# Prefix log-sum-exp over time: tiles of three time steps per partition instead of two, Exp written over its input, all tiles as one stream of chunks, and a last store in parts

## The chip, the cores and the metric

The kernel runs on one core of one Trainium2 chip. The metric is the device time of one execution in microseconds, as the median of several runs. The profile is one profiled execution on the same core.

## The reference

The input x has the shape (4, 4096, 4128) in float32: 4 batches, 4096 time steps, 4128 columns. For each batch and column the output is the running log-sum-exp over time:

```python
out[:, 0, :] = x[:, 0, :]
for t in range(1, S):
    mx = np.maximum(out[:, t - 1, :], x[:, t, :])
    out[:, t, :] = mx + np.log(np.exp(out[:, t - 1, :] - mx) + np.exp(x[:, t, :] - mx))
```

That is the logarithm of a running sum of exp(x). Input and output are 270.5 MB each, and both cross between HBM and the on-chip memory SBUF once.

## The kernel before

A tile is 256 consecutive time steps of one batch with all 4128 columns. It lies in SBUF as 128 partitions, each of which holds R = 2 consecutive time steps of 4128 columns, 33,024 bytes in one run. There are 16 tiles for each batch, 64 in all, and they are worked in order. A tile is loaded by one DMA (line 102) and stored by one DMA (line 153), both issued by SP, the sync engine. Five buffers `xt` hold tiles.

The columns of a tile are cut into four chunks of 1024; the last chunk also carries the 32 columns that are left over, called the tail. A chunk c goes through these steps in class `Step`:

- `exp(c)` (line 111): ScalarE (ACT) takes Exp of both time steps of the chunk and writes fp16 into a buffer `et`.
- `head(c)`: TensorE (PE) sums over the partitions with matmuls by constant 128x128 matrices. `incl` (a triangle with its diagonal) takes the first time step of every partition, `excl` (a triangle without it) the second, and `pick` adds the running sum that the tile before left in `carry[c]`. The result in `pt` (PSUM, the memory that PE writes) is the running sum at the first time step of each partition. Each chunk takes two matmuls of 512 columns for each matrix, line 86.
- `ln(0, c)` (line 126): ACT takes Ln of `pt` and writes it over `xt`, where the first time step was.
- `second(c)`: PE adds the second time step to `pt` by the unit matrix `ident`.
- `close(c)`: ACT takes Ln for the second time step, and then `keep` (lines 90 and 91) on VectorE (DVE) stores the last 32 partitions of `pt` as an fp16 value and an fp16 remainder in `carry[c]`. Two DVE instructions.

The tail has its own small matmuls (`tail_mm`), Ln (line 149) and carry.

The order is written out by hand in `run` and in the loop at the end. Within a tile, a chunk's Exp and head come one chunk ahead of the Ln of the chunk before. Between tiles nothing overlaps in this order: a tile's first Exp follows the last Ln of the tile before. On SP, three loads come first. For each tile i, the load of tile i + 3 is then issued ahead of the store of tile i. With five buffers that load waits until the store of tile i - 2 has ended.

Every matmul is issued with its own weight load (PEld in the profile).

Of the kernel before, what the change touches and what calls it, by code (L numbers as in the profile page):

```python
# [7 lines left out]
FP32 = mybir.dt.float32  # L8
FP16 = mybir.dt.float16
ACT = mybir.ActivationFunctionType  # L10
P = 128
R = 2
CH = 1024
MM = 512
HI, LO = 96, 32


def _constants(nc, pool):


    def tri(base, name):
        t = pool.tile([P, P], FP16, name=name)
        nc.gpsimd.memset(t, 1.0)

        nc.gpsimd.affine_select(  # L25
            out=t, in_=t, pattern=[[1, P]], compare_op=mybir.AluOpType.is_ge,
            fill=0.0, base=base, channel_multiplier=-1,
        )
        return t

    def ones_where_zero(bases, step, name):
        t = pool.tile([P, P], FP16, name=name)
        nc.gpsimd.memset(t, 0.0)
        for base in bases:
            nc.gpsimd.affine_select(  # L35
                out=t, in_=t, pattern=[[step, P]], compare_op=mybir.AluOpType.not_equal,
                fill=1.0, base=base, channel_multiplier=1,
            )
        return t

    return (
        tri(0, "incl"),
        tri(-1, "excl"),
        ones_where_zero([0], -1, "ident"),
        ones_where_zero([-(HI + 31), -(LO + 31)], 0, "pick"),
    )


@with_exitstack
def kernel(  # L50
    ctx: ExitStack,
    tc: tile.TileContext,
    x: bass.AP,
    out: bass.AP,
):

    nc = tc.nc
    B, S, D = x.shape  # L60
    rows = P * R
    n_t = S // rows
    assert S % rows == 0
    n_main = D // CH
    tail = D - n_main * CH
    t0 = n_main * CH

    nc.scalar.preload_act_table_set("natural_log_exp_and_others")  # L68
    consts = ctx.enter_context(tc.tile_pool(name="consts", bufs=1))
    incl, excl, ident, pick = _constants(nc, consts)  # L70

    xpool = ctx.enter_context(tc.tile_pool(name="xpool", bufs=5))
    epool = ctx.enter_context(tc.tile_pool(name="epool", bufs=4))
    cpool = ctx.enter_context(tc.tile_pool(name="cpool", bufs=1))
    pmain = ctx.enter_context(tc.tile_pool(name="pmain", bufs=3, space=bass.MemoryType.PSUM))
    ptail = ctx.enter_context(tc.tile_pool(name="ptail", bufs=2, space=bass.MemoryType.PSUM))

    carry = [cpool.tile([P, CH], FP16, name=f"carry{c}") for c in range(n_main)]
    carry_t = cpool.tile([P, tail], FP16, name="carry_t")
    for t in (*carry, carry_t):  # L80
        nc.vector.memset(t, 0.0)  # L81

    ctx.enter_context(tc.manual_schedule())

    def mm(pt, w, rhs, start, stop):
        nc.tensor.matmul(pt, lhsT=w, rhs=rhs, start=start, stop=stop, skip_group_check=True)  # L86

    def keep(cr, pt):

        nc.vector.tensor_copy(cr[HI:HI + 32, :], pt[HI:HI + 32])  # L90
        nc.vector.tensor_tensor(  # L91
            out=cr[LO:LO + 32, :], in0=pt[HI:HI + 32], in1=cr[HI:HI + 32, :],
            op=mybir.AluOpType.subtract,
        )

    class Step:
        def __init__(self, b, k):
            self.first = k == 0
            self.xt = xpool.tile([P, R, D], FP32, name="xt")
            self.et, self.pt = {}, {}  # L100
            self.dram = lambda t: t[b, k * rows:(k + 1) * rows, :].rearrange("(p j) d -> p j d", j=R)
            nc.sync.dma_start(out=self.xt, in_=self.dram(x))  # L102

        def cols(self, c):
            return slice(c * CH, (c + 1) * CH if c + 1 < n_main else D)

        def exp(self, c):
            s = self.cols(c)
            w = s.stop - s.start
            et = epool.tile([P, R, CH + tail], FP16, name="et")  # L110
            nc.scalar.activation(et[:, :, :w], self.xt[:, :, s], ACT.Exp)  # L111
            self.et[c] = et

        def head(self, c):
            et = self.et[c]
            pt = self.pt[c] = pmain.tile([P, CH], FP32, name="pt")
            for s in range(0, CH, MM):
                mm(pt[:, s:s + MM], incl, et[:, 0, s:s + MM], True, False)
            for s in range(0, CH, MM):
                mm(pt[:, s:s + MM], excl, et[:, 1, s:s + MM], False, self.first)  # L120
            if not self.first:
                for s in range(0, CH, MM):
                    mm(pt[:, s:s + MM], pick, carry[c][:, s:s + MM], False, True)

        def ln(self, j, c):
            nc.scalar.activation(self.xt[:, j, c * CH:(c + 1) * CH], self.pt[c], ACT.Ln)  # L126

        def second(self, c):
            pt = self.pt[c]
            for s in range(0, CH, MM):  # L130
                mm(pt[:, s:s + MM], ident, self.et[c][:, 1, s:s + MM], False, True)

        def close(self, c):

            self.ln(1, c)
            keep(carry[c], self.pt[c])

        def tail_mm(self):
            et = self.et[n_main - 1]
            qt = self.qt = ptail.tile([P, R, tail], FP32, name="qt")  # L140
            e0, e1 = et[:, 0, CH:], et[:, 1, CH:]
            for j in range(R):
                mm(qt[:, j, :], incl, e0, j == 0, False)
                mm(qt[:, j, :], incl if j else excl, e1, False, self.first)
                if not self.first:
                    mm(qt[:, j, :], pick, carry_t, False, True)

        def ln_tail(self):
            nc.scalar.activation(self.xt[:, :, t0:D], self.qt, ACT.Ln)  # L149
            keep(carry_t, self.qt[:, 1, :])  # L150

        def store(self):
            nc.sync.dma_start(out=self.dram(out), in_=self.xt)  # L153

        def run(self):
            last = n_main - 1
            self.exp(0)
            self.head(0)
            for c in range(1, n_main):
                self.exp(c)  # L160
                self.head(c)
                if c == last:
                    self.tail_mm()
                self.ln(0, c - 1)
                self.second(c - 1)
                if c >= 2:
                    self.close(c - 2)
            self.ln(0, last)
            self.second(last)
            self.close(last - 1)  # L170
            self.ln_tail()
            self.close(last)
            self.store()

    work = [(b, k) for b in range(B) for k in range(n_t)]
    ahead = 3
    steps = []
    for i, (b, k) in enumerate(work):
        if i == 0:
            steps += [Step(*work[n]) for n in range(ahead)]  # L180
        if i + ahead < len(work):
            n = i + ahead
            steps.append(Step(*work[n]))
        steps[i].run()


# [28 lines left out]
```

The softmax here doesn't subtract the row's maximum and nothing guards it: scores larger than these inputs give would overflow.

## Time and profile before

| what | value |
|---|---|
| median of 9 runs | 1265.41 us (1264.98 to 1266.11) |
| the profiled execution's own time | 1265.23 us |
| its span in the trace | 1263.4 us |
| bytes read and written | 270.53 MB each, 428 GB/s over the span |
| ACT busy | 962.4 us (76%), 833 instructions |
| PE busy | 660.6 us (52%), 2392 matmuls, and 2392 weight loads |
| DVE busy | 655.7 us (52%), 645 instructions |
| Exp of a chunk (128x2048) | 1904 ns each, 192 of them |
| Ln of a chunk's time step (128x1024) | 1028 ns each, 512 of them |
| `keep`, two instructions (32x1024) | 1230 and 1226 ns |
| a load | 4128 KB, 29.4 us from issue to landing |
| a store | 4128 KB, 38.9 us from issue to landing |

The span runs from the first to the last event of the trace; the execution's own time has a little more around it. A busy share says how much of the span an engine worked, and not whether it was waited for. A load's or a store's time from issue to landing holds its wait in the queue: 16 DMA engines share each transfer, and transfers issued earlier come first.

### The profile page before, as it was taken

How to read it: one execution, taken by the hardware profiler on the slowest of the kernel's cores; microseconds unless marked ns; L12 is line 12 of the kernel's file. 1: busy time of each engine (PE TensorE's matmuls, PEld its weight loads, DVE VectorE, ACT ScalarE, POOL GpSimd, SP SyncE). 2: the span in 40 equal slices, each digit the busy share in tenths (PEclk: the TensorE clock that was granted, in tenths of full speed). 3: DMA queues.
4: the chain of work that ended last, by engine and by line, in shares of the span. 5: the costliest groups of instructions: out<-in, count | busy, mean ns of one | idle time of the engine just before them, and what ended most of it. 6: DMA issues, size and time to landing. Idle time of an engine off the chain costs nothing.

```text
span 1263.4 us, 7025 instructions
## 1 busy us (share of the span) xinstructions
PE 660.6 (52%) x2392; PEld 242.4 (19%) x2392; DVE 655.7 (52%) x645; ACT 962.4 (76%) x833; POOL 2.2 (0%) x13
## 2 busy tenths in 40 slices
PE   2565655545545465464454655546445464554641
PEld 1222221211112121121121211112112121121210
DVE  3565565464454554545546455454564544545443
ACT  6889887778778787786877877778778787787872
POOL 0000000000000000000000000000000000000000
PEclk9878778777687776877767777777777787777776
DMA  9999999999999999999999999999999999999997
GB/s 401 417 433 433 429 432 434 429 431 430 433 434 433 433 432 433 429 433 431 434 434 433 435 428 432 431 435 430 434 435 434 433 433 431 429 433 431 434 434 328
DMA packets 18466, 541.51 MB, mean 429 GB/s; under 512 B 2048, under 2 KB 2048, under 8 KB 2048
## 3 DMA queue, kind: packets, MB, share of 16 engines
q1 hardware_dynamic: 18432, 541.07, 99.5%
q8 instruction: 19, 0.31, 0.1%
q14 instruction: 15, 0.12, 0.0%
HBM read 270.53 MB, written 270.53 MB: 428 GB/s over the span
## 4 chain that ended last, share of the span: by engine, by line
DMA 82%; ACT 1%; SPq 1%; DVE 1%; issue 1%; PE 0%; ACTq 0%
DMA out_dram<-xt 80%; DMA xt<-in_x_dram 2%; SPq L102 1%; ACT xt L126 1%; ACT et L111 1%; DVE carry L90 0%; DVE carry L91 0%; PE pt L86 0%; SPq L153 0%; DVE carry_t L90 0%; DVE carry_t L91 0%; ACTq L126 0%
## 5 line engine op out<-in xcount | busy, mean ns | idle before, releaser
L90 DVE CAST carry<-pt 32x1024 f16<-32x1024 f32 x256 | 314.8, 1230 | 574.7 <-ACT xt L126 571.4
L111 ACT ACTIVATE et<-xt 128x2048 f16<-128x2048 f32 (+1 forms) x256 | 485.5, 1921 | 152.4 <-DMA xt<-in_x_dram 152.4
L126 ACT ACTIVATE xt<-pt 128x1024 f32<-128x1024 f32 x512 | 504.4, 1028 | 124.5 <-PE pt L86 63.7
L86 PE MATMUL pt<-et,incl 128*128 128x512 f16 x512 | 210.9, 504 | 550.0 <-ACT et L111 375.2
L91 DVE TENSOR_TENSOR carry<-pt,carry 32x1024 f16<-32x1024 f32 x256 | 314.0, 1226 | 8.9
L86 PE MATMUL pt<-et,excl 128*128 128x512 f16 x512 | 210.9, 504 | 0.0
L86 PEld LDWEIGHTS <-incl 128*128 128x128 f16 x704 | 69.1, 111 | 684.0 <-issue 632.6
L86 PE MATMUL pt<-carry,pick 128*128 128x512 f16 x480 | 194.9, 498 | 0.0
L86 PE MATMUL pt<-et,ident 128*128 128x512 f16 x512 | 172.6, 422 | 28.3 <-ACT xt L126 28.3
L86 PEld LDWEIGHTS <-excl 128*128 128x128 f16 x576 | 71.0, 123 | 115.6 <-issue 82.9
L86 PEld LDWEIGHTS <-pick 128*128 128x128 f16 x600 | 69.7, 118 | 94.5 <-issue 66.0
L86 PEld LDWEIGHTS <-ident 128*128 128x128 f16 x512 | 49.5, 106 | 102.0 <-issue 75.5
L86 PE MATMUL qt<-et,incl 128*128 128x32 f16 x192 | 19.6, 189 | 0.0
L86 PE MATMUL qt<-carry_t,pick 128*128 128x32 f16 x120 | 15.6, 182 | 0.0
L149 ACT ACTIVATE xt<-qt 128x64 f32<-128x64 f32 x64 | 14.6, 227 | 0.0
L90 DVE CAST carry_t<-qt 32x32 f16<-32x32 f32 x64 | 12.6, 196 | 2.0
L91 DVE TENSOR_TENSOR carry_t<-qt,carry_t 32x32 f16<-32x32 f32 x64 | 12.4, 193 | 2.2
L86 PE MATMUL qt<-et,excl 128*128 128x32 f16 x64 | 11.6, 182 | 0.0
L81 DVE MEMSET carry<- 128x512 uint32 x4 | 1.9, 485 | 1.1 <-PEq L199 1.0
L68 ACT ACT_TABLE_LOAD x1 | 1.3, 1283 | 0.8 <-PEq L199 0.8
L35 POOL TENSOR_SCALAR_AFFINE_SELECT pick<-pick 128x128 f16<-128x128 f16 x2 | 0.6, 292 | 0.1
L25 POOL TENSOR_SCALAR_AFFINE_SELECT incl<-incl 128x128 f16<-128x128 f16 x1 | 0.3, 292 | 0.0
(11 smaller groups left out, 1.9 us busy)
## 6 DMA issues: line engine op xcount, KB each, us to landing
xt<-in_x_dram SPq DMA_DIRECT2D x64, 4128.0 KB, 29.4
out_dram<-xt SPq DMA_DIRECT2D x64, 4128.0 KB, 38.9
```

Of the source, the lines that this page charges most:

```text
L25: nc.gpsimd.affine_select(out=t, in_=t, pattern=[[1, P]], compare_op=mybir.AluOpType.is_ge, fill=0.0, base=base, channel_multiplier=-1,)
L35: nc.gpsimd.affine_select(out=t, in_=t, pattern=[[step, P]], compare_op=mybir.AluOpType.not_equal, fill=1.0, base=base, channel_multiplier=1,)
L68: nc.scalar.preload_act_table_set("natural_log_exp_and_others")
L81: nc.vector.memset(t, 0.0)
L86: nc.tensor.matmul(pt, lhsT=w, rhs=rhs, start=start, stop=stop, skip_group_check=True)
L90: nc.vector.tensor_copy(cr[HI:HI + 32, :], pt[HI:HI + 32])
L91: nc.vector.tensor_tensor(out=cr[LO:LO + 32, :], in0=pt[HI:HI + 32], in1=cr[HI:HI + 32, :], op=mybir.AluOpType.subtract,)
L102: nc.sync.dma_start(out=self.xt, in_=self.dram(x))
L111: nc.scalar.activation(et[:, :, :w], self.xt[:, :, s], ACT.Exp)
L126: nc.scalar.activation(self.xt[:, j, c * CH:(c + 1) * CH], self.pt[c], ACT.Ln)
L149: nc.scalar.activation(self.xt[:, :, t0:D], self.qt, ACT.Ln)
```

## The change

- A partition of a tile holds R = 3 consecutive time steps, a run of 49,536 bytes. A batch's 32 rows of 128 are ten tiles of three and one of two. In the first batch the tile of two comes first, in the others last. There are 44 tiles: 40 of three and 4 of two.
- Exp is written as fp16 over the first half of the chunk's own place in `xt`. The pool of `et` buffers is gone, and `xt` has four buffers of three rows.
- The chunks of all tiles are one list, 176 chunks. In turn g of one loop come: for chunk g - 2 the third Ln with `keep`, for chunk g - 1 the second Ln and the next `ident` matmuls, for chunk g the first Ln and its `ident` matmuls, then the Exp of chunk g + 2 and the head of chunk g + 1. This holds across the border of two tiles. A tile of two rows has two Ln, and `keep` follows the second.
- `head` takes the first row by `incl` and the other two by `excl`.
- `mm` gives `ldweights=False` where the matrix is the one of the matmul before.
- SP issues four loads first. Later a load follows a store: after the store of tile i comes the load of tile i + 3, into the buffer whose store was that of tile i - 1.
- The last store goes out as three DMAs, of partitions 0 to 4, 5 to 79 and 80 to 127.

```diff
-R = 2
+R = 3
+UNEVEN = ((0, 5), (5, 80), (80, P))
...
-    xpool = ctx.enter_context(tc.tile_pool(name="xpool", bufs=5))
-    epool = ctx.enter_context(tc.tile_pool(name="epool", bufs=4))
+    bufs = 4
+    xpool = ctx.enter_context(tc.tile_pool(name="xpool", bufs=bufs))
...
+    held = [None]
+
+    def mm(pt, w, rhs, start=False, stop=False):
+
+        if held[0] is not w:
+            nc.tensor.matmul(pt, lhsT=w, rhs=rhs, start=start, stop=stop, skip_group_check=True)
+            held[0] = w
+            return
+        pe = nc.tensor
+        pe.add_instruction(mybir.InstMatmult(
...
+            start_tensor_calc=start, stop_tensor_calc=stop, ldweights=False,
...
+        def store(self, parts=((0, P),)):
+            for a, b in parts:
+                nc.sync.dma_start(out=self.dram(out)[a:b], in_=self.xt[a:b])
...
+        def exp(self):
+            c0, w = self.c * CH, self.w
+            nc.scalar.activation(
+                self.t.half[:, :, 2 * c0:2 * c0 + w], self.t.xt[:, :, c0:c0 + w], ACT.Exp,
+            )
...
+        def stage(self, j):
+
+            t, c, pt = self.t, self.c, self.pt
+            nc.scalar.activation(t.xt[:, j, c * CH:(c + 1) * CH], pt, ACT.Ln)
+            if j + 1 < t.r:
+                for s in range(0, CH, MM):
+                    mm(pt[:, s:s + MM], ident, self.e(j + 1, s, s + MM), stop=j + 2 == t.r)
+                if c == last and j == 0:
+                    nc.scalar.activation(t.xt[:, :, t0:D], self.qt, ACT.Ln)
+                    keep(carry_t, self.qt[:, t.r - 1, :])
+            else:
+                keep(carry[c], pt)
...
+    ahead = bufs - 1
+    for s in steps[:bufs]:
+        s.load()
+    stored = 0
+    chunks[0].exp()
+    chunks[1].exp()
+    chunks[0].head()
+    for g in range(len(chunks) + R - 1):
+        for d in range(R - 1, -1, -1):
+            if 0 <= g - d < len(chunks) and d < chunks[g - d].t.r:
+                k = chunks[g - d]
+                k.stage(d)
+                if k.c == last and d + 1 == k.t.r:
+                    k.t.store(UNEVEN if k.t is steps[-1] else ((0, P),))
+                    if bufs <= stored + ahead < len(steps):
+                        steps[stored + ahead].load()
+                    stored += 1
+        if g + 2 < len(chunks):
+            chunks[g + 2].exp()
+        if g + 1 < len(chunks):
+            chunks[g + 1].head()
```

## The prediction

> **What bounds the kernel now.** I read the page's slices and queues first, then the chain that ended last, then the last 70 us in order of time, then short stretches of the end.
>
> ```profile
> DMA  9999999999999999999999999999999999999997
> GB/s 401 417 433 433 429 432 434 429 431 430 433 434 433 433 432 433 429 433 431 434 434 433 435 428 432 431 435 430 434 435 434 433 433 431 429 433 431 434 434 328
> ...
> q1 hardware_dynamic: 18432, 541.07, 99.5%
> ...
> DMA out_dram<-xt 80%; DMA xt<-in_x_dram 2%; SPq L102 1%; ACT xt L126 1%; ACT et L111 1%; DVE carry L90 0%; DVE carry L91 0%; PE pt L86 0%; SPq L153 0%; DVE carry_t L90 0%; DVE carry_t L91 0%; ACTq L126 0%
> ```
>
> All 16 DMA engines are full except in the first and last slice, and the chain is one store after another. ACT at 76% of the span, PE and DVE at 52% lie under it. The bytes do not change, so only three things can move the time: how fast a full DMA engine moves its bytes, a gap in the queue, and the end. The chain in order of time shows the end:
>
> ```profile
> 1193.82 29.40 DMA xt<-in_x_dram
> 1223.24 1.92 ACT et L111
> ```
>
> The last load lands at 1223.2 (call it T). SP's timeline then has the last store issued at 1240.15 (T + 16.9), while three older stores keep the queues full. Short stretches after that (columns: stretch, length, busy us of PE, PEld, DVE, ACT, POOL, clock, DMA share, GB/s):
>
> ```profile
> 1242.00:1252.00 10.00, 0.00 (x0) 0.00 (x0) 2.53 (x3) 0.00 (x0) 0.00 (x0) 0.50 1.03 446
> 1252.00:1254.00 2.00, 0.00 (x0) 0.00 (x0) 0.00 (x0) 0.00 (x0) 0.00 (x0) 0.50 0.69 297
> 1254.00:1256.00 2.00, 0.00 (x0) 0.00 (x0) 0.00 (x0) 0.00 (x0) 0.00 (x0) 0.50 0.69 297
> 1256.00:1258.00 2.00, 0.00 (x0) 0.00 (x0) 0.00 (x0) 0.00 (x0) 0.00 (x0) 0.50 0.31 132
> 1258.00:1260.00 2.00, 0.00 (x0) 0.00 (x0) 0.00 (x0) 0.00 (x0) 0.00 (x0) 0.50 0.12 50
> 1260.00:1262.00 2.00, 0.00 (x0) 0.00 (x0) 0.00 (x0) 0.00 (x0) 0.00 (x0) 0.50 0.04 17
> ```
>
> The engines do not stop together. In the trace's packet records, the last store's 16 completion packets fall so: five within 0.2 us, ten 2.4 to 6.5 us later, one 9.05 us after the first. This slow engine lost its 9 us over the whole run, some 0.14 us with each store. It never idles, and it ends at T + 39.3 (four times 9.76 us, the spacing of its DMAs), 0.9 us before the span's end.
>
> **What the Trainium skill says.** "DMA: Bandwidth & Descriptors", section Latency and other measured facts, calls engines 7 and 15 usually slower than the rest; here one engine of the 16 is. Its section on why a DMA increments its semaphore by 16 says that a transfer uses the largest k up to 16 that divides the partitions, on the lowest-numbered engines. The trace of before has 16 completion packets for each of its 128-partition DMAs, and no other k. The sections Where 436 GB/s comes from and How a descriptor splits into AXI transactions give prices below. "TensorE: Matmul & The Clock Gate" says that weight loads may run ahead of matmuls; here they do (PEld overlaps PE), so they are no wall time.
>
> **Part 1: runs of 49.5 KB.** DMAs fall from 128 to 88 full ones and three parts of one. Each engine still does 8 packets for each DMA. A full engine of before spends 9.757 us for 8 x 33,024 B; at the page's 27.2 GB/s an engine (435/16) the bytes alone are 9.713, so 0.044 us per DMA is overhead, and 40 fewer DMAs give -1.7 us. Against it: a row is 16,512 B, so two rows are 129 x 256 B, but three are 193.5 x 256 B, and every odd partition's run starts off a 256 B boundary. By the page this costs 4 beats of 32 B, 4.7 ns; four odd packets in each of 80 three-row DMAs make +1.5 us. The trace of before has only aligned runs. Bounds: 0 (the write side sets the pace) to +3.0 (both sides pay). I take +1.0. Sum: -0.7.
>
> **Part 2: one stream of chunks.** Three-row tiles need per chunk an Exp of 128x3072, by 1.5 x 1904 ns (the 128x2048 row) 2.86 us, and three Ln at 0.97 (pairs in the timeline take 1.93). Four chunks and the tail's Ln make 23.4 us of ACT per tile, and a load and a store take 2 x 14.6 = 29.2: hidden, with 6 us over. DVE's `keep` pairs fall from 256 to 176, 80 x 2.46 = 197 us less, all off the path. fp16 over x drops the et pool; loads now also wait for PE, whose reads end before the store that they wait for anyway. Cost 0.
>
> What the stream does add: ACT runs Exp two chunks ahead, so Exp of the next tile's first chunk stands before the last six Ln of this tile, and waits for the next load. A store now waits for the landing of the next tile. Worked along ACT's order: three Exp, seven Ln and the tail's Ln, 8.6 + 6.8 + 0.2 = 15.6 us after that landing. The slow engine then still has a store and a load before it, 29.2 us: no gap. The fast ones, 9 us ahead, need it 20.2 us after the landing less 1.3 us for a DMA to start (first issue 0.80, first packet 2.1): still in time. SP issues a load behind a store now; queued behind its wait is only the next store, which is not ready.
>
> **Part 3: held operands.** In the program as built, PE has 2,268 matmuls and still 2,268 weight loads, one for each; `ldweights=False` leaves none out. The 124 pairs fewer come from the three-row tiling. Cost 0, and were they gone, it would be 0 too: PE waits for ACT (375 us of its idle time before the incl matmuls).
>
> **Part 4: four loads up front.** Four loads are 23.2 MB, 54 us of queue. The first store waits for Exp of tile 1 and is ready near 37 us (landing 28.0, two Exp, four Ln), the second near 58: no gap, 0.
>
> **Part 5: the end.** Last come load 43 (two rows), stores 41, 42 (three rows) and 43 (two rows): 8 rows after the landing T, as before. But store 42 now waits for T: three Exp of 1.90, seven Ln and the tail's Ln, 5.7 + 6.8 + 0.2 = 12.7 us, and 1.3 to start. The fast engines are through store 41 at T - 9.05 + 14.6 = T + 5.6 (some 1.5 later if it too comes late to them, as the short load 43 before it makes it) and idle until T + 14.0; all but the slow one then start together and end store 42 at T + 28.6. Store 43 is issued near T + 24: in time by 3 us. Its parts of 5, 75 and 48 partitions use k = 5, 15 and 16 engines: engines 0 to 4 get 9 rows of 1.22 us, 5 to 14 get 8, engine 15 gets 3. If 15 is the slow one it ends at T + 29.2 + 3.7 = T + 32.9; the first five end last, at T + 28.6 + 11.0 = **T + 39.6**, against T + 39.3. So +0.3: what the split takes from the slow engine has been lost by the others' wait for store 42. T itself moves with part 1 and with the slow engine.
>
> Slow engine's own loss: 9 us before; bounds -3 (its delay is per packet, and packets fall by a third) to +1. I take 0.
>
> **Sum.** -1.7 + 1.0 + 0.3 = -0.4 us on the profiled execution's 1265.23 (span 1263.4 and 1.8 around it). The median of the runs shown is 1265.41, 0.2 above it. So **1264.9 us**.
>
> **Rivals.**
> - A, the slow engine loses per packet: -2.8 (9 us x 40/128), T comes earlier by it: 1262.1. For it: the delay sits in short extra times of single packets, all on stores. Against: such extra times may follow the work beside them, which lasts as long. Chance 0.13.
> - B, the split works as it is meant to: store 42 is issued early enough, nobody idles, and the last is the latest of the middle ten, T - 9.05 + 6.5 + 39.0 = T + 36.4, 2.9 before T + 39.3; with -0.7 of part 1, 1261.8. It needs store 42 some 8 us sooner than ACT's order gives. Chance 0.12.
> - C, slower: the odd partitions' runs. Each engine moves 320 of them. To be slower by 2.5 us they must eat 2.5 + 1.7 - 0.3 = 3.9 us, 12 ns each; from there it decides. At 16 ns (14 beats) it is 1265.4 - 1.7 + 5.1 + 0.3 = 1269.1. For it: stores of 128 B leftovers at both ends are not in the trace. Against: 14 beats is over three times the page's price. Chance 0.18.
> - D, compute too slow for the end: between the last two landings ACT has 14.6 + 9.8 = 24.4 us for 23.4 of work. An Exp over its own input of 3.5 us would take 26.0 and miss by 1.6; in store 42's chain its three two-row Exp are 2.33 instead of 1.90, 1.3 more: 1267.8. For it: no row shows Exp writing over its input. Against: 3.5 is 22% over the row. Chance 0.15; half of it is inside 0.2%.
> - Else my own case, 0.42, from 1262.5 to 1267.5.
>
> **How the numbers follow.** A measurement of this kernel tells a difference over about 0.2% (2.5 us) from none. Faster: A, B and a little of mine, 0.27. Slower: C, half of D and a little of mine, 0.31. Same: 0.42. The range reaches from 1260.0 (A and B partly together) to 1269.5 (C): cases of both signs; mine alone is 1262.5 to 1267.5.
>
> **What would show it.** DMA packets 8 per engine and DMA of 1.83 us each; 2,268 weight loads; a wait of the last full store for ACT after the last landing, with DMA's share falling 20 to 30 us before the end instead of only in the last 10; store 42 issued 12 to 13 us after that landing. A DMA spacing on a full engine over 14.65 us speaks for C, a slow engine that is under 7 us late for A, a last store that starts with the queues still full for B. The forecast is wrong if the time leaves 1260 to 1269.5, or if a gap opens in the middle of the run.

## The result, and the profile after

The changed kernel takes **1271.61 us** (median of 9 runs, 1271.39 to 1272.07) against 1265.39 us before (29 runs): a ratio of 1.0050, 95% interval 1.0042 to 1.0058. It is 6.2 us slower. The forecast was 1264.9 us, with a range from 1260.0 to 1269.5.

The page of the kernel after, with the lines that answer to those of before (engines' busy time, DMA share and rate by slice, the data queue, the chain by line):

```profile
PE 691.1 (54%) x2268; PEld 237.5 (19%) x2268; DVE 451.5 (36%) x445; ACT 947.3 (75%) x733; POOL 2.2 (0%) x13
...
DMA  9999999999999999999999999999999999999987
GB/s 408 420 436 423 440 427 434 435 425 440 431 426 445 426 437 431 429 442 431 428 433 434 435 426 445 425 430 441 430 429 432 437 427 437 434 432 434 427 364 283
...
q1 hardware_dynamic: 12692, 541.07, 99.0%
...
DMA xt<-in_x_dram 66%; ACT xt L146 10%; ACT xt L179 9%; DMA out_dram<-xt 5%; PE pt L99 3%; PE pt L95 1%; ACT xt L184 0%; DVE carry L109 0%; DVE carry L110 0%; SPq L134 0%; ACTq L248 0%; SPq L130 0%; ACTq L146 0%; PE qt L95 0%
```

The queue is full for 38 of the 40 slices, against 39 before. The chain now runs through loads, Exp and Ln where it ran from store to store: stores wait for the next tile's landing. The loss is in the last two slices. The timeline of the end shows the last landing released and the stores after it (start, length, engine, line, operation; the second line is store 42, the third the parts of store 43):

```profile
1220.89 1.91 ACT L146 ACTIVATE xt<-xt 128x2048 f16<-128x2048 f32 x1 [1.34 <-DMA xt<-in_x_dram]
...
1234.17 0.33 SPq L134 DMA_DIRECT2D out_dram<-xt  x1
...
1244.68 2.71 SPq L134 DMA_DIRECT2D out_dram<-xt  x3
```

Store 42 goes out 13.3 us after the landing. Two parts of the end, with the columns as before (the last two are DMA share and GB/s):

```profile
1228.00:1230.00 2.00, 0.80 (x3) 0.25 (x2) 0.36 (x1) 2.00 (x3) 0.00 (x0) 0.93 0.63 272
1230.00:1232.00 2.00, 1.11 (x4) 0.29 (x3) 1.97 (x2) 2.00 (x3) 0.00 (x0) 0.93 0.23 99
1232.00:1234.00 2.00, 2.00 (x6) 0.71 (x6) 0.13 (x1) 2.00 (x2) 0.00 (x0) 0.50 0.16 58
1234.00:1236.00 2.00, 0.93 (x3) 0.17 (x2) 1.79 (x2) 2.00 (x4) 0.00 (x0) 0.72 0.93 396
...
1250.00:1252.00 2.00, 0.00 (x0) 0.00 (x0) 0.00 (x0) 0.00 (x0) 0.00 (x0) 0.50 0.73 215
1252.00:1254.00 2.00, 0.00 (x0) 0.00 (x0) 0.00 (x0) 0.00 (x0) 0.00 (x0) 0.50 0.87 297
1254.00:1256.00 2.00, 0.00 (x0) 0.00 (x0) 0.00 (x0) 0.00 (x0) 0.00 (x0) 0.50 0.49 182
1256.00:1258.00 2.00, 0.00 (x0) 0.00 (x0) 0.00 (x0) 0.00 (x0) 0.00 (x0) 0.50 0.97 314
1258.00:1260.00 2.00, 0.00 (x0) 0.00 (x0) 0.00 (x0) 0.00 (x0) 0.00 (x0) 0.50 1.02 380
1260.00:1262.00 2.00, 0.00 (x0) 0.00 (x0) 0.00 (x0) 0.00 (x0) 0.00 (x0) 0.50 0.43 182
1262.00:1264.00 2.00, 0.00 (x0) 0.00 (x0) 0.00 (x0) 0.00 (x0) 0.00 (x0) 0.50 0.60 198
1264.00:1266.00 2.00, 0.00 (x0) 0.00 (x0) 0.00 (x0) 0.00 (x0) 0.00 (x0) 0.50 0.15 66
1266.00:1268.00 2.00, 0.00 (x0) 0.00 (x0) 0.00 (x0) 0.00 (x0) 0.00 (x0) 0.50 0.15 66
```

There are two dents. The first, 1228 to 1234, is the idle time of the fast engines ahead of store 42, where the prediction put it. The second was not foreseen: from 1250 on only the last store is under way, nothing computes, and the rate stays at 66 to 380 GB/s. In 1256 to 1260 the share is near 1 and the rate is only 314 and 380: engines are busy, but with packets that take too long. The packet records show it: of the 128 packets of 33,024 B (one row each) in that store, 28 take over 1.8 us and four of them 6.8 to 7.5, where 1.22 is usual. From its first packet to its last the store takes 19.3 us, against 10.6 in the run with a whole last store below. It has 36 completion packets, 5 + 15 + 16 for its three pieces, as the rule that the prediction took from the skill says.

A packet's record does not name its engine. But an engine's next packet mostly starts within 10 ns of the end of the one before, so the packets can be strung into 16 engines. Five of them move 1 + 5 + 3 = 9 rows of the last store; they are the prediction's engines 0 to 4. The packets of 6.80, 7.12, 7.27 and 7.50 us are the first rows of four of these five, and these four end last of all, at 1267.0 to 1269.3. The fifth is the slow engine: it ends store 42 at 1250.5, needs 1.22 us for its first row and is through at 1265.1. So the split gave the slow engine nine rows, the most of all, and not the three of engine 15.

Measured from the last landing T, the end came at T + 39.2 before (1262.4 less 1223.2; the prediction has 39.3), at T + 39.6 in the forecast and at T + 48.4 in the run (1269.3 less 1220.9). T itself came 2.3 us earlier than before.

### The profile page after: what moved, and what is told of

Same layout as the page of the kernel before. It is cut to its first block, busy times and chain, and to the rows that moved or that the text cites. A ratio compares the mean times of both kernels' runs of the same rounds, so it can differ in the third digit from the quotient of the medians.

```text
span 1270.4 us, 6167 instructions
## 1 busy us (share of the span) xinstructions
PE 691.1 (54%) x2268; PEld 237.5 (19%) x2268; DVE 451.5 (36%) x445; ACT 947.3 (75%) x733; POOL 2.2 (0%) x13
## 4 chain that ended last, share of the span: by engine, by line
DMA 71%; ACT 19%; PE 4%; issue 2%; DVE 1%; SPq 0%; ACTq 0%
DMA xt<-in_x_dram 66%; ACT xt L146 10%; ACT xt L179 9%; DMA out_dram<-xt 5%; PE pt L99 3%; PE pt L95 1%; ACT xt L184 0%; DVE carry L109 0%; DVE carry L110 0%; SPq L134 0%; ACTq L248 0%; SPq L130 0%; ACTq L146 0%; PE qt L95 0%
## 5 line engine op out<-in xcount | busy, mean ns | idle before, releaser
L146 ACT ACTIVATE xt<-xt 128x3072 f16<-128x3072 f32 (+3 forms) x176 | 478.2, 2717 | 247.2 <-DMA xt<-in_x_dram 247.2
L109 DVE CAST carry<-pt 32x1024 f16<-32x1024 f32 x176 | 216.4, 1230 | 760.5 <-ACT xt L179 760.2
L95 PE MATMUL pt<-xt,ident 128*128 128x512 f16 x176 | 77.6, 441 | 494.5 <-ACT xt L179 494.5
L99 PE MATMUL pt<-xt,ident 128*128 128x512 f16 x496 | 205.0, 481 | 34.2 <-ACT xt L179 34.0
L110 DVE TENSOR_TENSOR carry<-pt,carry 32x1024 f16<-32x1024 f32 x176 | 215.9, 1227 | 6.1
L99 PE MATMUL pt<-xt,excl 128*128 128x512 f16 x496 | 186.0, 493 | 0.0
L99 PEld LDWEIGHTS <-ident 128*128 128x128 f16 x496 | 51.3, 103 | 655.0 <-issue 642.0
L95 PE MATMUL pt<-xt,incl 128*128 128x512 f16 x176 | 92.9, 528 | 23.6 <-ACT xt L146 15.2
L99 PE MATMUL pt<-xt,incl 128*128 128x512 f16 x176 | 93.7, 532 | 0.0
L95 PE MATMUL pt<-xt,excl 128*128 128x512 f16 x176 | 93.5, 531 | 0.0
L99 PEld LDWEIGHTS <-excl 128*128 128x128 f16 x536 | 66.9, 125 | 104.0 <-issue 79.7
L95 PE MATMUL pt<-carry,pick 128*128 128x512 f16 x160 | 71.2, 445 | 0.0
L99 PE MATMUL pt<-carry,pick 128*128 128x512 f16 x160 | 68.2, 426 | 0.0
L95 PEld LDWEIGHTS <-excl 128*128 128x128 f16 x220 | 27.2, 123 | 37.0 <-issue 28.4
L95 PEld LDWEIGHTS <-pick 128*128 128x128 f16 x200 | 22.9, 114 | 29.9 <-issue 19.6
L99 PEld LDWEIGHTS <-pick 128*128 128x128 f16 x160 | 18.1, 113 | 28.1 <-issue 16.6
L95 PEld LDWEIGHTS <-ident 128*128 128x128 f16 x176 | 19.1, 108 | 21.8 <-issue 11.0
```

Of the source, the lines that this page charges most:

```text
L99: pe.add_instruction(mybir.InstMatmult(name=nc.get_next_instruction_name(), ins=[pe.lower_ap(rhs), pe.lower_ap(w, for_matmul_weights=True) ...
L110: nc.vector.tensor_tensor(out=cr[LO:LO + 32, :], in0=pt[HI:HI + 32], in1=cr[HI:HI + 32, :], op=mybir.AluOpType.subtract,)
L146: nc.scalar.activation(self.t.half[:, :, 2 * c0:2 * c0 + w], self.t.xt[:, :, c0:c0 + w], ACT.Exp,)
```

## The experiments

The theory: SBUF feeds DMA through ports, and pieces of neighbouring partitions leave a part of them unused. The Trainium skill has such a map, on the page "SBUF — State Buffer", section "Door 1: The DMA port swizzle (why `[64,N]` ≈ `[32,N]`)": 16 ports of 8 partitions each, partitions 0 to 63 on eight of them and 64 to 127 on the other eight. In a store of 128 partitions each engine has a port to itself. On that map partitions 0 to 3 share one port and partition 4 lies on another; in the first piece of the run above four rows took 6.8 us or more and one 1.22, which fits. (Four rows on one port would be 4.9 us by the usual 1.22; on the map rows 32 to 35 of the second piece use that port too.) Below this is theory P, and the ports that the expectations speak of are those of this map. Its rivals are the number of DMAs, and the unequal counts of rows. Each edit is to the changed kernel unless it says otherwise.

**The last store in one piece.**

```diff
-UNEVEN = ((0, 5), (5, 80), (80, P))
+UNEVEN = ((0, P),)
```

> The changed kernel with the last store as one DMA of 128 partitions; nothing else is changed. Theory P (ports: a store is fed by 16 SBUF ports of 8 partitions each, a port gives one engine's rate, and pieces of neighbouring partitions crowd on half of the ports): every engine has a port to itself again, the last store takes 8 x 1.22 = 9.8 us after store 42 instead of 18 to 19, and the kernel takes 1271.6 - 8.5 = 1263, 2 us below the kernel before. Rival N (the split is slow because it is three DMAs): also about 1263. Rival O (the over-long packets of the end come from something else, such as the writes of store 42 still under way): no change, 1271.

Measured: 1262.73 us, ratio to before 0.9980 (0.9973 to 0.9988). Stretches of the end:

```profile
1228.00:1230.00 2.00, 0.00 (x0) 0.00 (x0) 0.88 (x1) 2.00 (x4) 0.00 (x0) 1.00 0.74 322
1230.00:1232.00 2.00, 1.94 (x5) 0.60 (x5) 1.58 (x2) 2.00 (x3) 0.00 (x0) 0.54 0.12 50
1232.00:1234.00 2.00, 2.00 (x6) 0.68 (x5) 0.33 (x1) 2.00 (x3) 0.00 (x0) 0.61 0.10 33
1234.00:1236.00 2.00, 0.61 (x3) 0.10 (x1) 1.97 (x2) 2.00 (x3) 0.00 (x0) 1.00 0.93 396
...
1254.00:1256.00 2.00, 0.00 (x0) 0.00 (x0) 0.00 (x0) 0.00 (x0) 0.00 (x0) 0.50 1.18 512
1256.00:1258.00 2.00, 0.00 (x0) 0.00 (x0) 0.00 (x0) 0.00 (x0) 0.00 (x0) 0.50 1.22 528
1258.00:1260.00 2.00, 0.00 (x0) 0.00 (x0) 0.00 (x0) 0.00 (x0) 0.00 (x0) 0.50 0.04 17
```

(Shares over 1 come from packets being counted in the stretch where they start.) The first dent is still there, the second is gone: no packet of the last store takes over 1.23 us, and the engines end within 0.8 us of each other. The split alone costs 1271.61 - 1262.73 = 8.9 us, more than the whole loss. What is left of the change is 0.2% faster than before.

**Two halves with equal counts.**

```diff
-UNEVEN = ((0, 5), (5, 80), (80, P))
+UNEVEN = ((0, 64), (64, P))
```

> The changed kernel with the last store in two DMAs, partitions 0 to 63 and 64 to 127. Both use 16 engines with 4 rows each, so every engine has 8 rows as in one DMA. Theory P: each half lies on 8 ports, 8 rows a port, so each half takes 8 x 1.22 = 9.8 us and both 19.5: as slow as the changed kernel, 1271 to 1273, with packets of about 2.4 us. Rival C (unequal counts of rows, 9, 8 and 3, or k below 16, make the end late): counts are equal here, so about 1263. Rival N (number of DMAs): two instead of three, 1263 to 1268.

Measured: 1272.56 us (4 runs; ratio 1.0059, 1.0045 to 1.0073). Stretches of its end:

```profile
1252.00:1254.00 2.00, 0.00 (x0) 0.00 (x0) 0.00 (x0) 0.00 (x0) 0.00 (x0) 0.50 1.29 264
1254.00:1256.00 2.00, 0.00 (x0) 0.00 (x0) 0.00 (x0) 0.00 (x0) 0.00 (x0) 0.50 1.29 264
1256.00:1258.00 2.00, 0.00 (x0) 0.00 (x0) 0.00 (x0) 0.00 (x0) 0.00 (x0) 0.50 1.33 264
...
1266.00:1268.00 2.00, 0.00 (x0) 0.00 (x0) 0.00 (x0) 0.00 (x0) 0.00 (x0) 0.50 1.17 264
```

All engines are busy, each has 8 rows, and the rate is far below that of the whole store. The median packet takes 2.57 us, twice the usual, and the halves end at 1260.6 and 1270.3, 20 us after the store began. The store is as slow with equal counts, so unequal counts are not what makes it slow.

**Three pieces by columns.**

```diff
-UNEVEN = ((0, 5), (5, 80), (80, P))
+UNEVEN = ((0, P),)
...
+        def store_columns(self):
+            for a, b in ((0, 1376), (1376, 2752), (2752, D)):
+                nc.sync.dma_start(out=self.dram(out)[:, :, a:b], in_=self.xt[:, :, a:b])
...
-                    k.t.store(UNEVEN if k.t is steps[-1] else ((0, P),))
+                    k.t.store_columns() if k.t is steps[-1] else k.t.store()
```

> The changed kernel with the last store in three DMAs by columns (1376 of 4128 each), each over all 128 partitions: three DMAs as in the change, 16 packets of 5.5 KB per engine in each, every engine on its own port. Theory P: as one DMA, plus overhead of more packets (48 instead of 8, some 5 ns each, 0.2 us): 1263 to 1264. Rival N: as slow as the changed kernel, 1271.

Measured: 1263.45 us (ratio 0.9985, 0.9979 to 0.9992), 0.7 above the whole store. Three DMAs as such cost little; what costs is pieces by partitions.

**Three quarters and one quarter.**

```diff
-UNEVEN = ((0, 5), (5, 80), (80, P))
+UNEVEN = ((0, 96), (96, P))
```

> The changed kernel with the last store in two DMAs, partitions 0 to 95 and 96 to 127; 16 engines in both, 6 and 2 rows each. Theory P, counted out: partitions 0 to 63 are all 8 rows of one half of the ports, 64 to 95 are 4 rows on each of the other half, so the first piece takes 8 x 1.22 = 9.8 us and the second, 4 rows on each of 8 ports, 4.9: 14.7 in all against 9.8 of the whole store, 1262.7 + 4.9 = 1267.6, half way to the run with two halves. A rival in which every split by partitions costs the same, whatever the ports: 1272.

Measured: 1267.44 us (ratio 1.0017, 1.0010 to 1.0024). The count by ports gave 1267.6. Two stretches of its end:

```profile
1254.00:1256.00 2.00, 0.00 (x0) 0.00 (x0) 0.00 (x0) 0.00 (x0) 0.00 (x0) 0.50 1.00 363
1256.00:1258.00 2.00, 0.00 (x0) 0.00 (x0) 0.00 (x0) 0.00 (x0) 0.00 (x0) 0.50 1.01 314
```

The penalty over the whole store is 4.7 us here, 9.8 with two halves: with these two cuts it follows the rows that the fullest port has in each piece. For the three pieces of the change the same count is 4 + 8 + 8 rows, by an estimate from the map 24.4 us if one piece followed the other; the store took 19.3, since engines start on a piece while others are still busy with the one before. There the count is only a bound.

Within the first piece of this run the two paces stand side by side. Five engines end their six rows by 1257.3, close to 1.22 us a row; the other eleven, which began with them at 1249.4 to 1250.2, end no earlier than 1259.6. Six rows for each engine, in the order of the partitions, put partitions 66 to 95 on five engines, all in the half with four rows a port. A cause that slows a whole piece alike, on the side of HBM for instance, would not divide the engines so.

**The split alone, on the kernel before.**

```diff
+UNEVEN = ((0, 5), (5, 80), (80, P))
...
+            self.last = (b, k) == (B - 1, n_t - 1)
...
-            nc.sync.dma_start(out=self.dram(out), in_=self.xt)
+            parts = UNEVEN if self.last else ((0, P),)
+            for a, b in parts:
+                nc.sync.dma_start(out=self.dram(out)[a:b], in_=self.xt[a:b])
```

> The kernel before with only its last store split into partitions 0 to 4, 5 to 79 and 80 to 127. There the engines reach the last store up to 9 us apart, as the split was made for. Theory P: the pieces crowd on the ports all the same, some 8 to 9 us more than the 9.8 of a whole store, partly under the slow engine's lag: 1268 to 1271. Rival C (row counts decide; in the prediction's words, rival B: the split works where nobody has waited): the slow engine is relieved of 5 rows, the last is the latest of the middle ten, 1265.4 - 2.6 = 1262.8.

Measured: 1273.14 us (4 runs, 1271.16 to 1274.4; ratio 1.0062, 1.0048 to 1.0075), 2 to 5 us more than expected and about as slow as the changed kernel. The split costs 7.8 us where no engine has waited for a store.

It does not test rival B as it was meant to, for the slow engine is not relieved of five rows. Strung into engines, the packets of this run show that the engine which reaches the last store last moves 1 + 5 + 3 rows of it, nine and not three. It comes there at 1259.6, where it came at 1252.6 without the split: while the others were in the pieces of the last store, one of its rows of the store before took 4.7 us. Its nine rows then last until 1271.7, 12.1 us instead of 9.8. Together these are the 9.3 us by which the last packet comes later than before (1271.7 against 1262.4) in this run, the slowest of the four. What a split does that gives the slow engine three rows is not shown.

**Two rows instead of three** (with the whole last store).

```diff
-R = 3
+R = 2
```

> The kernel of the whole last store with R = 2: one stream of chunks, fp16 over x, four buffers and four loads up front, but two time steps per partition, 128 DMAs of 33,024-byte runs as before. Theory: the three-row runs give only the overhead of DMAs left out, 40 x 0.044 = 1.7 us, so here the spacing of DMAs on an undisturbed engine is 9.757 us again and the time 1262.7 + 1.7 = 1264.5. Rival: runs of 49.5 KB cost or give more (odd partitions start off a 256 B boundary, which the prediction priced at 1.0): then the time is as in the kernel of the whole last store or lower, 1261 to 1263.

Measured: 1268.00 us (ratio 1.0023, 1.0013 to 1.0032), 3.5 above the theory. The theory's term holds: the spacing of DMAs on an undisturbed engine is 9.757 us, against 14.613 for three rows, which is 0.022 us less for the same bytes. The end is another. The timeline has the Exp that the last landing released:

```profile
1233.21 1.91 ACT L146 ACTIVATE xt<-xt 128x2048 f16<-128x2048 f32 x1 [3.45 <-DMA xt<-in_x_dram]
```

and two stretches after it:

```profile
1252.00:1254.00 2.00, 0.59 (x2) 0.10 (x1) 1.90 (x4) 1.32 (x3) 0.00 (x0) 1.00 0.00 0
1254.00:1256.00 2.00, 0.00 (x0) 0.00 (x0) 1.77 (x3) 0.33 (x1) 0.00 (x0) 0.74 0.61 264
```

With two rows the three stores after the last landing are 29 us of queue. With three rows they are 39, since two of them are larger, and the landing is earlier, at 1220.8 in the run with a whole last store. So the last tile's Ln is covered with three rows. With two the slowest engine ends the store before the last at 1252.7 and the last store's first packet is at 1255.5: the queue is dry for some 2.7 us while ACT, PE and DVE work, most of the 3.5. The tile size matters here through what covers the end more than through the run length.

**Store 42 sooner** (with the whole last store): the Exp of the last tile's chunks one chunk ahead instead of two.

```diff
-        if g + 2 < len(chunks):
+        if g + 2 < len(chunks) - n_main:
             chunks[g + 2].exp()
+        if len(chunks) - n_main <= g + 1 < len(chunks):
+            chunks[g + 1].exp()
```

> The kernel of the whole last store in which the Exp of the last tile's chunks comes one chunk ahead of its Ln instead of two, so that less stands between the last landing and store 42: two Exp, four Ln, about 8 us instead of 13.3. Theory: the time is set by the slow DMA engine, which never waits for store 42, and the fast engines' idle time of 7 us costs nothing: 1262.7 within 0.5, with the DMA share falling some 5 us less. Rival: the end is set by that wait: 1262.7 - 5 = 1258.

Measured: 1263.05 us (ratio 0.9983, 0.9975 to 0.9990). Store 42 went out at 1231.52 instead of 1233.66, 2 us sooner and not 5, as the PE work between Exp and Ln is now waited for. The time did not follow: the first dent is shorter, and the slow engine still ends last, at 1260.2 against 1260.1. So 2 us of the fast engines' idle time cost nothing, and that all of it is free is not shown beyond this.

**No `keep`** (with the whole last store): DVE's carries are left out, so each tile starts from zero and the output is not the reference's.

```diff
-                    keep(carry_t, self.qt[:, t.r - 1, :])
...
-                keep(carry[c], pt)
+                pass
```

> The kernel of the whole last store without the DVE instructions that keep the running sum: each tile starts from zero, and DVE does nothing after its first memsets. Asks what makes one DMA engine late by 0.18 us with every three-row store. Theory D (DVE's work disturbs that engine's stores): the slow engine is no later than the middle ones, 5 us, and the end comes up to 3 us earlier, 1260. Rival (another engine's work, or none): its lag at the last landing stays at 7 to 8 us and the time at 1262.7. Without carries PE and ACT have the same instructions.

Measured: 1261.78 us (ratio 0.9972, 0.9961 to 0.9982), 1 us below the whole store. The latest engine is 7.1 us behind the first at the last landing, against 7.4 with `keep`. DVE's carries explain at most 0.3 us of that lag; where the 1 us comes from is open.

**The carry's remainder in other partitions** (with the whole last store).

```diff
-HI, LO = 96, 32
+HI, LO = 96, 64
```

> The kernel of the whole last store with the carry's remainder in partitions 64 to 95 instead of 32 to 63 (the two constants of `pick` follow). Theory D of the run without keep, in its form that DVE's writes crowd on the slow engine's partitions: the lag grows or moves to other engines, the time changes by 1 us or more. Rival: nothing changes, 1262.7 within 0.5.

Measured: 1262.79 us (ratio 0.9981, 0.9973 to 0.9989), no change, and the lag at the last landing is 7.3. What delays one engine's stores stays open.

## Why the prediction was wrong

The step that failed is in part 5: "engines 0 to 4 get 9 rows of 1.22 us, 5 to 14 get 8, engine 15 gets 3 ... the first five end last, at T + 28.6 + 11.0". The counts of rows were right. The 1.22 us a row, measured in stores of all 128 partitions, does not hold for pieces of 5, 75 and 48: there engines share ports. The first rows of four of the five engines took 6.8 to 7.5 us, and the store 19.3 us instead of 11.0. That is 8.3 us, and the forecast missed by 6.7; most of the rest is what came out better than planned at T. The whole store, the columns, the three quarters and the halves agree on the cause in size: 0, 0.7, 4.7 and 9.8 us over the whole store. The prediction asked only how many engines a piece has, not which ports its partitions lie on.

That the first five did end last is luck: four of them did so for their long first rows, while the fifth, with nine rows too, was through 4 us before the last.

The split also rested on "If 15 is the slow one". It is not: in the run of the changed kernel and in that of the split on the kernel before, the slow engine is one of the five that get nine rows. Even at 1.22 us a row the split would have given it one row more, 1.2 us, and not five fewer. Rival B needs it to be engine 15, so neither run is its case.

The other steps:

- The bound was right: a full queue until the end, and the end decides.
- Part 1, the overhead: its figures give 14.61 us for a three-row DMA without a price for misaligned runs (1.5 times 9.713, and 0.044), and 14.613 is the most common spacing in the run. The 1.0 us for odd partitions was wrong: of 10,240 three-row packets 8,376 took exactly 1,829 ns and 785 took 1,833 to 1,835, where a price of 4.7 ns on every odd partition would put half of them. The price that the prediction took from the Trainium skill, "DMA: Bandwidth & Descriptors", section How a descriptor splits into AXI transactions, does not show in these runs. Rival C falls with it. The count is one off: 87 full DMAs and three parts, not 88 and three, which changes the sum by less than 0.1 us.
- Part 2: no gap in mid-run, as worked out. Exp of 128x3072 took 2767 ns (forecast 2860), writing over its own input, so rival D falls.
- Part 3: 2,268 matmuls and 2,268 weight loads, in the first line of the page above.
- Part 4: the first stores were in time, no gap.
- Part 5 up to store 42: issued at T + 13.3 (forecast 12.7), the fast engines idle for 7 us, all but the slow one then together. With the last store whole the end is T + 39.3, and the same sum with 8 rows for every engine gives T + 38.4 for the fast and T + 39.0 for the slow one. It is the term for the parts that broke.
- The slow engine came 7.4 us late at the last landing, against 8.7 before. On each three-row store it loses some 0.18 us, against 0.14 on two rows. A loss per packet would have left about 6 us, a loss by bytes 8.7: the lag fell by about half of what rival A says.
- T came 2.3 us earlier, not 0.7: about 1.1 from the fast engines' pace and about 1.3 from the smaller lag.

## What to carry to other kernels

Split a store by columns, or not at all: a piece that holds only some of the partitions can leave ports idle while every DMA engine counts as busy, so look at GB/s beside the DMA share, and at the length of single packets. Before giving a late engine fewer rows, find out which one it is: here the split gave it the most. When a stream couples a tile's store to the next tile's landing, count at the end of the run what queued work still covers it: of the versions here that compute the whole result, the one with the whole last store and three rows, 1262.73 us, is the best, level with its two variants at 1262.79 and 1263.05.

## What the hardware showed that was not expected

- A store in two halves, partitions 0 to 63 and 64 to 127, makes packets of 2.57 us (median) where 1.22 is usual, and a rate of 264 GB/s while every engine is busy. With pieces of 5, 75 and 48 partitions four of the first five rows took 6.8 to 7.5 us.
- Of runs of 49,536 B every second one starts, by its size, 128 B off a 256 B boundary. Eight of them took an engine 14.613 us, no more than 1.5 times the 9.757 of eight aligned runs of 33,024 B.
- One engine of 16 loses 0.14 to 0.18 us with each store while compute runs, at most 0.03 with a load, and nothing once compute has ended. Leaving out DVE's `keep` lowers its lag by only 0.3 us of 7.4, moving the carry's remainder by 0.1.
